# TensorE's instructions kept in the order of the program, from the first to the last

## The chip, the cores and the metric

The kernel runs on one core of a Trainium2 chip. The metric is device microseconds per execution, and lower is better. The kernel before takes 317.19 us, the median of 3 runs (316.95 to 317.62).

## The reference

One decoder layer on 256 tokens of width 1024, in float32. One input projection feeds two groups of eight heads of width 64. Group A is stick-breaking attention, group B a dilated sliding-window softmax attention whose three windows are merged by their denominators. Every head's output is RMS-normalised with a gain; an output projection, a residual and a LayerNorm follow, then a SwiGLU feed-forward of inner width 2816 with a second residual and LayerNorm.

```python
proj = jnp.einsum('bsd,dn->bsn', h, w_in[l])
q_a, k_a, v_a, q_b, k_b, v_b = jnp.split(proj, split_at, axis=-1)
o_a = stick_breaking_attention(_heads(q_a), _heads(k_a), _heads(v_a))
o_b = dilated_window_attention(_heads(q_b), _heads(k_b), _heads(v_b), slopes)
mixed = jnp.concatenate([_head_rms_merge(o_a, g_sb[l]), _head_rms_merge(o_b, g_dil[l])], axis=-1)
h = _layer_norm(ALPHA * h + jnp.einsum('bsm,md->bsd', mixed, w_out[l]), ln1_g[l], ln1_b[l])
gate = jnp.einsum('bsd,df->bsf', h, w_gate[l])
up = jnp.einsum('bsd,df->bsf', h, w_up[l])
ffn = jnp.einsum('bsf,fd->bsd', jax.nn.silu(gate) * up, w_down[l])
h = _layer_norm(ALPHA * h + ffn, ln2_g[l], ln2_b[l])
```

## The kernel before

**Products.** Every operand of a projection is split in two parts, `hi` (rounded to the matmul's own type, by ScalarE) and `lo` (the rest, by VectorE); `split` at line 78 does that. A product is three matmuls, hi by hi, hi by lo and lo by hi (`prod`, line 223). Weights come in chunks of 128x2048, which the class `Weights` loads and splits a piece at a time between other work: the tiles `wraw`, `whi` and `wlo` in the trace.

**Stages.** Heads are worked in eight pairs. Pairs 0 to 3 are group A, pairs 4 to 7 group B. `qk_proj` projects queries and keys of one pair into a PSUM bank with tag `in` (the tile `p_in`), and `v_proj` projects values into banks with the same tag. There are two such banks, used in turn. `evacuate` (line 253) copies the bank out: ScalarE writes `padhi` twice and `oh`, VectorE writes `padlo` twice and `ol`, which is the last reader. Then come scores, weights, values (line 363, the tile `o`) and `normalise` (line 384), which makes `mh` and `ml`, the pair's part of the output projection's input. The output projection of the first 128 tokens adds up in `acc0`, two banks with tag `in` (line 525), that of the other 128 in `acc1`, two banks with tag `big`. The first bank of `acc0` takes the place of pair 6's `p_in`, the second that of pair 7's. A LayerNorm of 128 tokens (`norm1`, line 567) is transposed on TensorE (tile `tr`, two rounds of four) for the feed-forward. The first three feed-forward chunks are computed by token (`ff_by_token`, line 617) and their gated product is transposed (tile `pt`); the rest by channel. The down projection and the second LayerNorm end the kernel.

**What sets the order.** The program is not written stage after stage: a small planner, the class `Order` (line 408), keeps a clock of its own while the program is traced. `fill` emits one product of a long projection and adds its cost; a follow-up step (scores, weights, values, normalise, transposes) is queued with a lag by `after` and emitted by the first `fill` at which its time has come. `drain` emits what is left. That gives the order of the program. After it, the framework's scheduler arranges each engine's instructions by its own estimate of when they are ready. It leaves alone those marked by `tc.keep_in_program_order`. The class `Pinned` (line 62) marks what is issued through `pe`, `act_e` and `dve`, while its class variable `on` holds: `step1` (line 454) clears it once scores of a pair other than 0 are emitted, so at pair 1's. From there the scheduler is free. Instructions written as `nc.tensor...`, such as the stick-breaking weights' (line 311), the transposes' and the values', are never marked.

```python
            return lambda *a, **k: tc.keep_in_program_order(f(*a, **k)) if Pinned.on else f(*a, **k)

            x1 = scores(j, pad, plain)
            Pinned.on = Pinned.on and j == 0
```

Of the kernel before, what the change touches and what calls it, by code (L numbers as in the profile page):

```python
# [47 lines left out]
def decoder_layer(ctx: ExitStack, tc: tile.TileContext, first, x, wqk, wv, wo, wgu, wd,  # L48
                  gmix, lnrows, biases, out):
    nc = tc.nc  # L50
# [11 lines left out]
    class Pinned:  # L62

        on = True

        def __init__(self, engine):
            self.engine = engine

        def __getattr__(self, name):
            f = getattr(self.engine, name)  # L70
            return lambda *a, **k: tc.keep_in_program_order(f(*a, **k)) if Pinned.on else f(*a, **k)  # L71

    pe, act_e, dve = Pinned(nc.tensor), Pinned(nc.scalar), Pinned(nc.vector)

    def bank(tag, name):
        return ps.tile([128, 512], F32, tag=tag, name=name)

    def split(src, hi, lo):
        act_e.activation(hi, src, AF.Copy)
        dve.tensor_sub(lo, src, hi)  # L80
# [93 lines left out]
    for i in range(4):  # L174
        r = wp.tile([128, 2048], F32, tag="wraw", name="wraw", bufs=NRAW)
# [5 lines left out]
    idle = cst.tile([128, 128], BF16, name="idle")  # L181
    nc.vector.memset(idle, 0.0)
    warm = bank("o", "warm")
    for _ in range(NWARM):
        nc.tensor.matmul(warm.rearrange("p (r n) -> p r n", r=4), idle,  # L185
                         idle[:, None, :].to_broadcast([128, 4, 128]), start=True, stop=True, skip_group_check=True)


# [2 lines left out]
    ident = cst.tile([128, 128], F32, name="ident")  # L191
    identb = cst.tile([128, 128], BF16, name="identb")
    maskb = cst.tile([128, 128], BF16, name="maskb")
    blkr = cst.tile([128, 128], F32R, name="blkr")
# [10 lines left out]
    for h in range(2):  # L205
        r = slice(h * 64, h * 64 + 64)
# [16 lines left out]
    def prod(dst, lhs, rhs, start, stop):  # L223

        pe.matmul(dst, lhs[0], rhs[0], start=start, stop=False, skip_group_check=True)
        pe.matmul(dst, lhs[0], rhs[1], start=False, stop=False, skip_group_check=True)
        pe.matmul(dst, lhs[1], rhs[0], start=False, stop=stop, skip_group_check=True)
# [45 lines left out]
    def heads(t, n):  # L273
        return t[:, :2 * n].rearrange("p (h n) -> p h n", h=2)
# [30 lines left out]
    def stick_weights(z0, z1, sph, spl):  # L305
        z0d = z0.rearrange("p (h n) -> p h n", h=2)
        for sp in (sph, spl):
            s1 = sp[:, 512:768]
            for dst, lhs, rhs in ((z0, negtri, sp[:, 0:512]), (z0d[:, :, 128:256], negones, heads(s1, 128)),
                                  (z1[:, :256], negtri, s1)):  # L310
                nc.tensor.matmul(dst, lhs, rhs, start=False, stop=True, skip_group_check=True)  # L311
        w0 = at.tile([128, 512], F32, tag="w0", name="w0")
        w1 = at.tile([128, 256], F32, tag="w1", name="w1")
        nc.scalar.activation(w0, z0, AF.Exp)
        nc.scalar.activation(w1, z1[:, :256], AF.Exp)
        return w0, w1
# [32 lines left out]
    def dilated_weights(e0, e1):  # L349
        t0 = bank("big", "t0")  # L350
        t1 = bank("sml", "t1")
        for h in range(2):
            nc.tensor.transpose(t0[:, h * 256:h * 256 + 128], e0[:, h * 128:h * 128 + 128], ident)
        for h in range(2):
            nc.tensor.transpose(t0[:, h * 256 + 128:h * 256 + 256], e1[:, h * 256:h * 256 + 128], ident)
            nc.tensor.transpose(t1[:, h * 128:h * 128 + 128], e1[:, h * 256 + 128:h * 256 + 256], ident)
        w0 = at.tile([128, 512], F32, tag="w0", name="w0")
        w1 = at.tile([128, 256], F32, tag="w1", name="w1")
        nc.scalar.activation(w0, t0, AF.Copy)
        nc.vector.tensor_copy(w1, t1[:, :256])  # L360
        return w0, w1

    def values(j, w0, w1):

        g, pj = divmod(j, 4)
        o = bank("o", "o")
        for h in range(2):
            c = slice(pj * 128 + h * 64, pj * 128 + h * 64 + 64)
            r = slice(h * 64, h * 64 + 64)
            nc.tensor.matmul(o[r, 0:256], vt[g, 0][:, c], w0[:, h * 256:h * 256 + 256],  # L370
                             start=True, stop=False, skip_group_check=True)
        for h in range(2):
            c = slice(pj * 128 + h * 64, pj * 128 + h * 64 + 64)
            r = slice(h * 64, h * 64 + 64)
            nc.tensor.matmul(o[r, 128:256], vt[g, 1][:, c], w1[:, h * 128:h * 128 + 128],  # L375
                             start=False, stop=True, skip_group_check=True)
        sq = at.tile([128, S], F32, tag="sq", name="sq")
        nc.scalar.activation(sq, o[:, :S], AF.Square)
        sqh = at.tile([128, 2, S], F32R, tag="sqh", name="sqh")
        nc.scalar.activation(sqh[:, 0, :], o[:, :S], AF.Square)  # L380
        nc.vector.tensor_sub(sqh[:, 1, :], sq, sqh[:, 0, :])
        return o, sqh

    def normalise(j, o, sq):

        ms = o[:, S:2 * S]
        for i in range(2):
            nc.tensor.matmul(ms, blkr, sq[:, i, :], start=i == 0, stop=i == 1, skip_group_check=True)  # L388
        sq = at.tile([128, S], F32, tag="sq", name="sq")
        nc.scalar.activation(sq, ms, AF.Ln, bias=eps_rms)  # L390
        nc.scalar.activation(sq, sq, AF.Exp, scale=-0.5)
        nc.vector.scalar_tensor_tensor(sq, o[:, :S], gm[:, j:j + 1], sq, op0=ALU.mult, op1=ALU.mult)
        mh = cst.tile([128, S], F32R, tag=f"m{j}0", name="mh")
        ml = cst.tile([128, S], F32R, tag=f"m{j}1", name="ml")
        split(sq, mh, ml)
        mixed[j] = (mh, ml)
# [69 lines left out]
    vt, v_at = {}, {}  # L466
# [100 lines left out]
    def norm1(t, acc, lag):  # L567
        def after(c, h):
            n = c.start // 512

            def transposes():
                p = bank("sml", "tr")
                for i in range(4):
                    kt = n * 4 + i
                    nc.tensor.transpose(p[:, i * 128:i * 128 + 128],  # L575
                                        h[:, kt * 128:kt * 128 + 128], ident)
                pv = p.rearrange("p (k n) -> p k n", k=4)
                hi = xhi[:, n * 4:n * 4 + 4, t * 128:t * 128 + 128]
                lo = xlo[:, n * 4:n * 4 + 4, t * 128:t * 128 + 128]
                nc.scalar.activation(hi, pv, AF.Copy)  # L580
                nc.vector.tensor_sub(lo, pv, hi)
            od.after(lag + n * 0.66, 0.43, transposes)
        return layer_norm(acc, x_nat[:, t, :], rows1[:, 0, :], rows1[:, 1, :], x_nat[:, t, :], after, halves)
# [9 lines left out]
    def gated(g, u, shape, tag, dst=None):  # L593
        s = ff.tile(shape, F32, tag=tag, name="silu", bufs=3)
        nc.scalar.activation(s, g, AF.Silu)
        if dst is None:
            dst = s
        else:
            s, u = (v.rearrange("p (t n) -> p t n", t=2) for v in (s, u))
        nc.vector.tensor_mul(dst, s, u)  # L600
        return dst
# [15 lines left out]
    def ff_by_token(f, t, tag, last):  # L617
        w = weights.get(14 + f)
        tk = slice(t * 128, t * 128 + 128)
        p = bank(tag, "pg")  # L620
        for kt in range(KT):
            c = slice(kt * 256, kt * 256 + 256)
            od.fill(0.33, lambda: prod(p[:, :256], (xhi[:, kt, tk], xlo[:, kt, tk]), (w[0][:, c], w[1][:, c]),
                                       kt == 0, kt == KT - 1))
        with tc.issue_after(last):
            a = gated(p[:, 0:128], p[:, 128:256], [128, 128], "at")

        def transpose():
            q = bank("sml", "pt")
            nc.tensor.transpose(q[:, :128], a, ident)  # L630
            nc.scalar.activation(act[f][0][:, tk], q[:, :128], AF.Copy)
            nc.vector.tensor_sub(act[f][1][:, tk], q[:, :128], act[f][0][:, tk])
        od.after(LAG_ACT, 0.11, transpose)
# [195 lines left out]
```

## Time and profile before

| | before |
|---|---|
| median of 3 runs | 317.19 us |
| the profiled execution's own time | 316.86 us |
| its span, first to last instruction | 315.1 us |
| TensorE busy | 305.9 us, 97%, 2112 matmuls |
| VectorE busy | 240.6 us, 76% |
| ScalarE busy | 190.7 us, 61% |
| TensorE's share of the chain that ended last | 94% |
| mean granted clock of TensorE | 0.996 |

TensorE (PE in the rows) works through nearly the whole span. VectorE (DVE) and ScalarE (ACT) prepare its operands. Times in the rows count from the start of the span. A timeline row gives the start and the time of an instruction until its result is there; matmuls of a row overlap, so the next one starts earlier than the row before it ends. An "x2" behind a row means that two instructions, which follow each other closely, are shown as one.

### The profile page before, as it was taken

How to read it: one execution, taken by the hardware profiler on the slowest of the kernel's cores; microseconds unless marked ns; L12 is line 12 of the kernel's file. 1: busy time of each engine (PE TensorE's matmuls, PEld its weight loads, DVE VectorE, ACT ScalarE, POOL GpSimd, SP SyncE). 2: the span in 40 equal slices, each digit the busy share in tenths (PEclk: the TensorE clock that was granted, in tenths of full speed). 3: DMA queues.
4: the chain of work that ended last, by engine and by line, in shares of the span. 5: the costliest groups of instructions: out<-in, count | busy, mean ns of one | idle time of the engine just before them, and what ended most of it. 6: DMA issues, size and time to landing. Idle time of an engine off the chain costs nothing.

```text
span 315.1 us, 5440 instructions
## 1 busy us (share of the span) xinstructions
PE 305.9 (97%) x2112; PEld 277.8 (88%) x2112; DVE 240.6 (76%) x465; ACT 190.7 (61%) x406; POOL 4.1 (1%) x22
## 2 busy tenths in 40 slices
PE   8999999999999999999999999999999999999990
PEld 4988898799997778999999999999999988888880
DVE  4778998659897479997646466585597699999765
ACT  5789997777787458666446364473542675565011
POOL 5000000000000000000000000000000000000000
PEclk9999999999999999999999999999999999999998
DMA  7979887297332104789455464563613253630011
GB/s 255 399 301 381 277 283 263 113 358 292 151 137 69 64 2 133 249 294 370 157 189 214 139 226 172 166 235 133 218 50 136 80 188 130 270 135 0 0 67 67
DMA packets 9657, 58.02 MB, mean 184 GB/s; under 512 B 1184, under 2 KB 1440, under 8 KB 3360
## 3 DMA queue, kind: packets, MB, share of 16 engines
q1 hardware_dynamic: 9344, 57.22, 49.8%
q10 hardware_dynamic: 288, 0.46, 0.4%
q8 instruction: 16, 0.26, 0.3%
q14 instruction: 9, 0.07, 0.1%
HBM read 56.63 MB, written 1.05 MB: 183 GB/s over the span
## 4 chain that ended last, share of the span: by engine, by line
PE 94%; DVE 2%; ACT 1%; DMA 1%; issue 0%; DVEq 0%
PE pg L71 40%; PE p_in L71 22%; PE d L71 15%; PE acc L71 7%; PE z L71 2%; PE o L370 1%; PE s L71 1%; PE warm L185 1%; PE z L311 1%; DVE y L563 1%; PE o L375 1%; DVE bst L548 1%; DMA out_h<-y 1%; DVE y L546 1%; PE o L388 1%; PE tr L575 1%
## 5 line engine op out<-in xcount | busy, mean ns | idle before, releaser
L71 DVE TENSOR_TENSOR wlo<-wraw,whi 128x512 fp32r<-128x512 f32 (+2 forms) x194 | 138.0, 739 | 37.9 <-ACT whi L71 37.0
L71 ACT ACTIVATE whi<-wraw 128x512 fp32r<-128x512 f32 (+2 forms) x194 | 121.2, 671 | 58.0 <-PE pg L71 35.2
L71 PE MATMUL pg<-xhi,whi 128*128 128x256 f32 x304 | 85.7, 282 | 0.0
L71 PE MATMUL pg<-xlo,whi 128*128 128x256 f32 x304 | 85.5, 281 | 0.0
L71 PE MATMUL pg<-xhi,wlo 128*128 128x256 f32 x304 | 85.5, 281 | 0.0
L71 PEld LDWEIGHTS pg<-xhi,whi 128*128 128x128 f32 x304 | 57.2, 188 | 0.0
L71 PEld LDWEIGHTS pg<-xlo,whi 128*128 128x128 f32 x304 | 57.2, 188 | 0.0
L71 PEld LDWEIGHTS pg<-xhi,wlo 128*128 128x128 f32 x304 | 57.2, 188 | 0.0
L71 PE MATMUL p_in<-xhi,whi 128*128 128x256 f32 x128 | 36.5, 286 | 0.0
L71 PE MATMUL p_in<-xhi,wlo 128*128 128x256 f32 x128 | 36.3, 283 | 0.0
L71 PE MATMUL p_in<-xlo,whi 128*128 128x256 f32 x128 | 36.1, 282 | 0.0
L71 PE MATMUL d<-whi,s 128*128 128x512 f32 x84 | 26.9, 395 | 0.0
L71 PE MATMUL d<-whi,a 128*128 128x512 f32 (+1 forms) x92 | 25.9, 363 | 0.0
L71 PEld LDWEIGHTS p_in<-xhi,whi 128*128 128x128 f32 x128 | 24.1, 188 | 1.4 <-issue 0.7
L71 PEld LDWEIGHTS p_in<-xlo,whi 128*128 128x128 f32 x128 | 24.1, 188 | 0.2
L71 PEld LDWEIGHTS p_in<-xhi,wlo 128*128 128x128 f32 x128 | 24.1, 188 | 0.1
L71 PEld LDWEIGHTS d<-whi,s 128*128 128x128 f32 x84 | 15.8, 188 | 3.8
L71 PEld LDWEIGHTS d<-whi,a 128*128 128x128 f32 x92 | 16.6, 189 | 2.9
L71 PE MATMUL d<-wlo,a 128*128 128x512 f32 (+1 forms) x46 | 16.7, 363 | 0.0
L71 PE MATMUL d<-wlo,s 128*128 128x512 f32 x42 | 16.6, 395 | 0.0
L71 ACT ACTIVATE s<-slots 128x896 fp32r<-128x896 f32 x6 | 5.7, 953 | 13.4 <-DVE slots L611 13.4
L71 PE MATMUL pg<-wlo,xhi 128*128 128x256 f32 x48 | 13.6, 286 | 0.0
(151 smaller groups left out, 473.7 us busy)
## 6 DMA issues: line engine op xcount, KB each, us to landing
wraw<-in_wgu SPq DMA_DIRECT2D x22, 1024.0 KB, 4.8
wraw<-in_wd SPq DMA_DIRECT2D x11, 1024.0 KB, 4.8
wraw<-in_wqk SPq DMA_DIRECT2D x6, 1024.0 KB, 5.7
wraw<-in_wo SPq DMA_DIRECT2D x4, 1024.0 KB, 4.7
wraw<-in_first SPq DMA_DIRECT2D x8, 384.0 KB, 6.3
wraw<-in_wv SPq DMA_DIRECT2D x3, 1024.0 KB, 5.4
rows<-in_lnrows SPq DMA_DIRECT2D x2, 1024.0 KB, 6.6
wraw<-in_wv SPq DMA_DIRECT2D x2, 512.0 KB, 7.0
```

The lines of the kernel that those rows point to most:

```text
L71: return lambda *a, **k: tc.keep_in_program_order(f(*a, **k)) if Pinned.on else f(*a, **k)
L185: nc.tensor.matmul(warm.rearrange("p (r n) -> p r n", r=4), idle, idle[:, None, :].to_broadcast([128, 4, 128]), start=True, stop=True, ski ...
L311: nc.tensor.matmul(dst, lhs, rhs, start=False, stop=True, skip_group_check=True)
L370: nc.tensor.matmul(o[r, 0:256], vt[g, 0][:, c], w0[:, h * 256:h * 256 + 256], start=True, stop=False, skip_group_check=True)
L375: nc.tensor.matmul(o[r, 128:256], vt[g, 1][:, c], w1[:, h * 128:h * 128 + 128], start=False, stop=True, skip_group_check=True)
L388: nc.tensor.matmul(ms, blkr, sq[:, i, :], start=i == 0, stop=i == 1, skip_group_check=True)
L546: nc.vector.scalar_tensor_tensor(y[:, c], res[:, c], scale, acc[i][:, :c.stop - c.start], op0=ALU.mult, op1=ALU.add)
L548: nc.vector.bn_stats(st[:, i, :], y[:, c])
L563: nc.vector.scalar_tensor_tensor(dst[:, c], y[:, c], r[:, 3:4], b[:, c], op0=ALU.mult, op1=ALU.add)
L575: nc.tensor.transpose(p[:, i * 128:i * 128 + 128], h[:, kt * 128:kt * 128 + 128], ident)
```

## The change

`Pinned` takes a second argument, `always`. TensorE's wrapper is made with it, so it marks each instruction whatever `Pinned.on` says. ScalarE's and VectorE's wrappers are as before. The matmuls and transposes that were written as `nc.tensor...` are written as `pe...`. No instruction is added or taken away, and no lag or cost of the planner is changed. ScalarE's and VectorE's unmarked instructions are still arranged by the scheduler, which now arranges them around another order on TensorE.

```diff
-        def __init__(self, engine):
+        def __init__(self, engine, always=False):
             self.engine = engine
+            self.always = always
 
         def __getattr__(self, name):
             f = getattr(self.engine, name)
-            return lambda *a, **k: tc.keep_in_program_order(f(*a, **k)) if Pinned.on else f(*a, **k)
-
-    pe, act_e, dve = Pinned(nc.tensor), Pinned(nc.scalar), Pinned(nc.vector)
+            return lambda *a, **k: tc.keep_in_program_order(f(*a, **k)) if self.always or Pinned.on else f(*a, **k)
+
+    pe, act_e, dve = Pinned(nc.tensor, True), Pinned(nc.scalar), Pinned(nc.vector)
...
-                nc.tensor.matmul(dst, lhs, rhs, start=False, stop=True, skip_group_check=True)
+                pe.matmul(dst, lhs, rhs, start=False, stop=True, skip_group_check=True)
...
-            nc.tensor.matmul(ms, blkr, sq[:, i, :], start=i == 0, stop=i == 1, skip_group_check=True)
+            pe.matmul(ms, blkr, sq[:, i, :], start=i == 0, stop=i == 1, skip_group_check=True)
...
-            nc.tensor.transpose(q[:, :128], a, ident)
+            pe.transpose(q[:, :128], a, ident)
```

The other lines of the diff put `pe` for `nc.tensor` in the same way: the idle matmuls at the start, the transposes of the dilated weights, the values and the transposes of the first LayerNorm.

**Place one: pair 1's stick-breaking weights, on TensorE.** `sph` and `spl` are the two parts of the logarithms, written by VectorE; `p_in_410` is the value projection of the second 128 tokens and `p_in_469` pair 2's projection. A number behind a name tells tiles of one name apart, and the square brackets name the engines whose work an instruction waits for. Before:

```order
L71 MATMUL p_in_410<-whi_321,xlo_72 128x512
L311 MATMUL z0_368<-sph_378,negtri_99 128x512 [waits DVE_49]
L311 MATMUL z0_368<-sph_378,negones_98 128x2x128
L311 MATMUL z1_369<-sph_378,negtri_99 128x256
L71 MATMUL p_in_410<-whi_321,xhi_71 128x512
L71 MATMUL p_in_410<-wlo_322,xhi_71 128x512
L71 MATMUL p_in_410<-whi_321,xlo_72 128x512
L71 MATMUL p_in_469<-xhi_71,whi_364 128x256 [waits Activation_49]
L71 MATMUL p_in_469<-xlo_72,whi_364 128x256
L311 MATMUL z0_368<-spl_379,negtri_99 128x512 [waits DVE_49]
L311 MATMUL z0_368<-spl_379,negones_98 128x2x128
L311 MATMUL z1_369<-spl_379,negtri_99 128x256
```

The same stretch of TensorE in the changed kernel:

```order
L72 MATMUL p_in_410<-whi_321,xlo_72 128x512
L72 MATMUL z0_368<-sph_378,negtri_99 128x512 [waits DVE_49]
L72 MATMUL z0_368<-sph_378,negones_98 128x2x128
L72 MATMUL z1_369<-sph_378,negtri_99 128x256
L72 MATMUL z0_368<-spl_379,negtri_99 128x512 [waits DVE_49]
L72 MATMUL z0_368<-spl_379,negones_98 128x2x128
L72 MATMUL z1_369<-spl_379,negtri_99 128x256
L72 MATMUL p_in_410<-whi_321,xhi_71 128x512
L72 MATMUL p_in_410<-wlo_322,xhi_71 128x512
L72 MATMUL p_in_410<-whi_321,xlo_72 128x512
```

The six matmuls stand together now, and the group on `sph` stands three matmuls of 128x512 further ahead than before. The five matmuls that stood between the two groups come after both.

**Place two: the start of the output projection, on TensorE.** `acc0_1236` and `acc0_1237` are the two banks of the first 128 tokens, `mh_528` and `mh_541` the normalised pairs 0 and 1, `t0_1256` the transposes of pair 6's weights and `s0_1278` pair 7's scores. Before:

```order
L71 MATMUL acc0_1236<-whi_1027,mh_528 128x512 [waits PE_49]
...
L71 MATMUL acc0_1236<-whi_1027,mh_541 128x512
...
L353 MATMUL t0_1256<-ident_100,e_1179 128x128 [waits DVE_49,PE_49]
...
L370 MATMUL o_1302<-w0_1264,v10_727 64x256 [waits Activation_49]
...
L375 MATMUL o_1302<-w1_1265,v11_786 64x128 [waits DVE_49]
L71 MATMUL s0_1278<-padhi1_281,oh_1228 128x256 [waits PE_49,Activation_49]
...
L71 MATMUL acc0_1237<-whi_1027,mh_528 128x512 [waits DVE_49,PE_49]
...
L71 MATMUL s0_1278<-padhi1_281,ol_1229 128x256
L71 MATMUL s1_1279<-padhi1_281,ol_1229 128x512
L375 MATMUL o_1302<-w1_1265,v11_786 64x128
```

The same stretch of TensorE in the changed kernel:

```order
L72 MATMUL acc0_1236<-whi_1027,ml_529 128x512
L72 MATMUL acc0_1237<-whi_1027,mh_528 128x512 [waits DVE_49,PE_49]
...
L72 MATMUL acc0_1236<-whi_1027,mh_541 128x512
...
L72 MATMUL t0_1256<-ident_100,e_1179 128x128 x3
...
L72 MATMUL s0_1278<-padhi1_281,oh_1228 128x256 [waits Activation_49]
...
L72 MATMUL o_1302<-w0_1264,v10_727 64x256 [waits Activation_49]
```

The first matmul of `acc0_1237` is now the fourth of the stage, ahead of pair 6's transposes and pair 7's scores; it was the twenty-fourth. Groups that were cut in two (pair 7's scores, pair 6's values) stand whole.

**Place three: the end of the output projection of the first 128 tokens, on TensorE.** `mh_1367` and `mh_1408` are the normalised pairs 6 and 7, `o_1385` pair 7's values and, with `blkr`, its mean of squares; `acc1` is the other 128 tokens. Before:

```order
L71 MATMUL acc0_1237<-whi_1315,ml_1275 128x512
L370 MATMUL o_1385<-w0_1357,v10_727 64x256 [waits Activation_49]
...
L71 MATMUL acc1_1416<-whi_1027,mh_528 128x512 [waits PE_49]
...
L71 MATMUL acc1_1417<-whi_1027,mh_528 128x512 [waits PE_49]
L71 MATMUL acc0_1236<-whi_1342,mh_1367 128x512 [waits Activation_49]
...
L388 MATMUL o_1385<-sqh_1392,blkr_103 128x256 [waits DVE_49]
L71 MATMUL acc1_1417<-wlo_1028,mh_528 128x512
...
L71 MATMUL acc1_1416<-whi_1145,mh_808 128x512
L71 MATMUL acc0_1236<-whi_1342,mh_1408 128x512 [waits Activation_49]
```

The same stretch of TensorE in the changed kernel:

```order
L72 MATMUL acc0_1237<-whi_1315,ml_1275 128x512
L72 MATMUL acc0_1236<-whi_1342,mh_1367 128x512 [waits Activation_49]
...
L72 MATMUL acc0_1236<-whi_1342,ml_1368 128x512 [waits DVE_49]
L72 MATMUL o_1385<-w0_1357,v10_727 64x256 x2
...
L72 MATMUL o_1385<-sqh_1392,blkr_103 128x256 [waits DVE_49]
L72 MATMUL acc0_1236<-whi_1342,mh_1408 128x512 [waits Activation_49]
...
L72 MATMUL acc1_1416<-whi_1027,mh_528 128x512 [waits PE_49]
```

Thirteen matmuls of `acc1` stood between pair 7's values and the first matmul on `mh_1408`, four of them ahead of the one on `mh_1367`. All of them stand behind `acc0` now, and `mh_1367` is wanted ahead of pair 7's values. Further on, TensorE's transposes of the first LayerNorm stand 14 matmuls of 128x512 earlier than before, and the transposes `pt` of the first three feed-forward chunks stand where the planner put them, that of the third chunk right behind the chunk's last product.

## Rows read from the trace of the kernel before

**Rows 1.** Chain of waits, whole span; columns: start, length, what ran, how many.

```profile
29.37 2.10 PE p_in L71 x9
...
107.78 0.22 PE o L375 x4
...
123.32 7.72 PE pg L71 x65
...
145.18 105.02 PE pg L71 x885
```

**Rows 2.** Timeline of TensorE, pair 1's weights; start, time, line, output<-inputs.

```profile
31.31 0.40 PE L311 MATMUL z<-sph,negtri 128*128 128x512 f32 x1
...
32.71 0.39 PE L311 MATMUL z<-spl,negtri 128*128 128x512 f32 x1
```

**Rows 3.** Timeline of VectorE, the two parts of pair 1's logarithms.

```profile
30.17 0.55 DVE L301 CAST sph<-ab 128x768 fp32r<-128x768 f32 x1
...
31.24 0.95 DVE L302 TENSOR_TENSOR spl<-ab,sph 128x768 fp32r<-128x768 f32 x1
```

**Rows 4.** Timeline of TensorE, start of the output projection; brackets: idle before, releaser.

```profile
94.11 0.39 PE L71 MATMUL acc<-whi,mh 128*128 128x512 f32 x1
...
97.21 0.65 PE L370 MATMUL o<-w,v 128*64 128x256 f32 x4 [0.22 <-ACT w L359]
...
100.62 0.43 PE L375 MATMUL o<-w,v 128*64 128x128 f32 x2
```

**Rows 5.** Timeline of ScalarE, pair 7's evacuation.

```profile
97.41 0.39 ACT L71 ACTIVATE oh<-p_in 128x256 fp32r<-128x256 f32 x1
```

**Rows 6.** Timeline of VectorE, pair 7's evacuation.

```profile
96.56 0.43 DVE L71 SCALAR_TENSOR_TENSOR padlo<-p_in,padhi 64x256 fp32r<-64x256 f32 x1
...
97.48 0.69 DVE L71 TENSOR_TENSOR wlo<-wraw,whi 128x512 fp32r<-128x512 f32 x1
98.09 0.42 DVE L71 SCALAR_TENSOR_TENSOR ol<-p_in,oh 128x256 fp32r<-128x256 f32 x1
```

**Rows 7.** Timeline of TensorE, pairs 6 and 7 at the projection's end.

```profile
106.80 0.39 PE L71 MATMUL acc<-whi,ml 128*128 128x512 f32 x1
...
107.61 0.39 PE L375 MATMUL o<-w,v 128*64 128x128 f32 x4
...
110.36 0.41 PE L388 MATMUL o<-sqh,blkr 128*128 128x256 f32 x2
```

**Rows 8.** Timeline of ScalarE, pair 7's normalised part.

```profile
112.28 0.42 ACT L71 ACTIVATE mh<-sq 128x256 fp32r<-128x256 f32 x1 [0.55 <-DVE sq L392]
```

**Rows 9.** Timeline of VectorE, normalising pairs 6 and 7.

```profile
107.63 0.48 DVE L392 SCALAR_TENSOR_TENSOR sq<-o,gm,sq 128x256 f32<-128x256 f32 x1 [0.91 <-ACT sq L391]
...
109.10 0.42 DVE L381 TENSOR_TENSOR sqh<-sq,sqh 128x256 fp32r<-128x256 f32 x1
...
112.73 0.42 DVE L71 TENSOR_TENSOR ml<-sq,mh 128x256 fp32r<-128x256 f32 x1 [0.48 <-ACT mh L71]
```

**Rows 10.** Timeline of VectorE, the second half's first LayerNorm and first gated product.

```profile
124.53 0.66 DVE L546 SCALAR_TENSOR_TENSOR y<-x_nat,acc 128x512 f32<-128x512 f32 x1
...
126.92 0.20 DVE L550 BATCH_NORM_AGGREGATE mv<-bst 128x2 f32<-128x12 f32 x1
...
128.92 1.41 DVE L563 SCALAR_TENSOR_TENSOR x_nat<-y,rs,rows 128x512 f32<-128x512 f32 x2
130.33 0.49 DVE L600 TENSOR_TENSOR silu<-silu,pg 128x128 f32<-128x128 f32 x2
```

**Rows 11.** Timeline of ScalarE, one gate of the feed-forward.

```profile
136.19 0.28 ACT L595 ACTIVATE silu<-pg 128x128 f32<-128x128 f32 x1 [0.67 <-PE pg L71]
```

**Rows 12.** Windows: length, each engine's busy time, granted clock (PEclk), DMA share, GB/s.

```profile
307.30:312.30 5.00, 0.00 (x0) 0.00 (x0) 4.38 (x10) 1.46 (x6) 0.00 (x0) 1.00 0.05 20
312.40:315.00 2.60, 0.00 (x0) 0.00 (x0) 0.00 (x0) 0.00 (x0) 0.00 (x0) 0.50 0.43 149
```

**Rows 13.** Timeline of TensorE, the idle matmuls at the start.

```profile
1.05 4.35 PE L185 MATMUL warm<-idle 128*128 128x512 bf16 x10 [1.05 <-DVE idle L182]
```

More of the change, by code (lines that the diff above doesn't have):

```diff
@@ L184, in decoder_layer @@
     for _ in range(NWARM):
-        nc.tensor.matmul(warm.rearrange("p (r n) -> p r n", r=4), idle,
+        pe.matmul(warm.rearrange("p (r n) -> p r n", r=4), idle,
                          idle[:, None, :].to_broadcast([128, 4, 128]), start=True, stop=True, skip_group_check=True)
@@ L352, in dilated_weights @@
         for h in range(2):
-            nc.tensor.transpose(t0[:, h * 256:h * 256 + 128], e0[:, h * 128:h * 128 + 128], ident)
+            pe.transpose(t0[:, h * 256:h * 256 + 128], e0[:, h * 128:h * 128 + 128], ident)
         for h in range(2):
-            nc.tensor.transpose(t0[:, h * 256 + 128:h * 256 + 256], e1[:, h * 256:h * 256 + 128], ident)
-            nc.tensor.transpose(t1[:, h * 128:h * 128 + 128], e1[:, h * 256 + 128:h * 256 + 256], ident)
+            pe.transpose(t0[:, h * 256 + 128:h * 256 + 256], e1[:, h * 256:h * 256 + 128], ident)
+            pe.transpose(t1[:, h * 128:h * 128 + 128], e1[:, h * 256 + 128:h * 256 + 256], ident)
         w0 = at.tile([128, 512], F32, tag="w0", name="w0")
@@ L369, in values @@
             r = slice(h * 64, h * 64 + 64)
-            nc.tensor.matmul(o[r, 0:256], vt[g, 0][:, c], w0[:, h * 256:h * 256 + 256],
+            pe.matmul(o[r, 0:256], vt[g, 0][:, c], w0[:, h * 256:h * 256 + 256],
                              start=True, stop=False, skip_group_check=True)
@@ L374, in values @@
             r = slice(h * 64, h * 64 + 64)
-            nc.tensor.matmul(o[r, 128:256], vt[g, 1][:, c], w1[:, h * 128:h * 128 + 128],
+            pe.matmul(o[r, 128:256], vt[g, 1][:, c], w1[:, h * 128:h * 128 + 128],
                              start=False, stop=True, skip_group_check=True)
@@ L574, in transposes @@
                     kt = n * 4 + i
-                    nc.tensor.transpose(p[:, i * 128:i * 128 + 128],
+                    pe.transpose(p[:, i * 128:i * 128 + 128],
                                         h[:, kt * 128:kt * 128 + 128], ident)
```

## The prediction

> **What bounds the kernel now.** I read the chain of waits first. For 105 us after 145.18, 885 feed-forward matmuls follow one another with nothing between them [rows 1], and the chain reads so nearly all the way from the first projection to the second LayerNorm. TensorE is the bound, and it hardly waits for anyone: the longest idle time that its timeline names is 0.22 us [rows 4]. From that follows how the change is costed. No matmul is added or removed, so TensorE's work is the same, and since it has no slack, a microsecond that it waits longer is a microsecond on the end. I then set the two orders side by side, and at each place where an instruction came forward I read when its operand was there and when TensorE would now reach it.
>
> A matmul of 128x512 takes 0.23 us on TensorE (nine in 2.10), one of 128x256 in the feed-forward 0.119 (65 in 7.72) [rows 1]. An operand's result is handed over some 0.05 us after the writer's row ends; that is my estimate, from gaps of 0.03 to 0.05 between such rows.
>
> **Place one, pair 1's weights.** The matmuls on `sph` began at 31.31 [rows 2]; three matmuls of 128x512 earlier is 31.31 - 0.69 = 30.62. VectorE ends `sph` at 30.17 + 0.55 = 30.72 [rows 3], so TensorE waits until 30.77: 0.15. The three matmuls on `sph` take 0.47 (one of 128x512, two of half the width), which brings it to 31.24. `spl` ends at 31.24 + 0.95 = 32.19 [rows 3], handed over at 32.24: a wait of 1.00. Before, five other matmuls stood in that gap and the first on `spl` came at 32.71 [rows 2], when it was ready. VectorE's list up to `spl` is the same in both orders, so this chain doesn't move. Cost **1.15**, from 1.1 to 1.4: the upper end is for pair 0's and 1's normalisation, in front of which the scheduler now puts one or two more weight pieces on VectorE.
>
> **Place two, the second bank.** `acc0_1237` takes the bank that pair 7's projection left, so it waits for the last reader, `ol` on VectorE. The stage begins at 94.11 [rows 4]; after three matmuls TensorE reaches it at 94.80. When is `ol` done? Before, at 98.09 + 0.42 = 98.51 [rows 6], with `oh` at 97.41 [rows 5], because pair 6's copies stood in front. In the new order ScalarE does `oh` ahead of them, and VectorE's list is: second `padlo`, one weight piece, `ol`. The second `padlo` starts at 96.56 and ends at 96.99; the weight piece takes 0.61 to the next start (97.48 to 98.09), so `ol` runs from about 97.5 to 97.95 [rows 6]. Wait: 98.0 - 94.8 = **3.2**. Bounds: 2.6 if `ol` follows `padlo` at once (97.4), 3.7 if it ends where it did.
> Something is given back here. Behind the wait all operands are ready: pair 6's transposes come 3.2 us later than their weights need, and so do the scores. TensorE's wait for pair 6's copy `w` goes, 0.22 us [rows 4] and about 0.15 for resuming. The groups that were cut in two are whole: two lone value matmuls took 0.36 to 0.43 [rows 4], where four in one group take 0.22 [rows 1]. That makes 0.5; more switches of operand kind may add as much. I take 0.7, out of 0.2 to 1.0. Net **2.5**, from 1.6 to 3.5.
>
> **Place three, pairs 6 and 7.** Three waits, counted on the clock of before.
> First, `mh_1367` is wanted right after pair 5's part: at 106.80 + 0.23 = 107.03 [rows 7]. VectorE's step before it ends at 107.63 + 0.48 = 108.11 [rows 9]; `mh` adds 0.42 [rows 8], so 108.58 with the handovers: a wait of 1.55. `ml` comes 0.45 behind [rows 8, 9], just when two matmuls have run.
> Second, pair 7's mean of squares needs both halves of `sqh`. Before, VectorE wrote the second 109.10 + 0.42 - 107.61 = 1.9 us after the last value matmuls began [rows 7, 9], with pair 6's `mh` and `ml` in between. Those are out of the way, which saves some 0.4, while TensorE has only three matmuls and the first half (1.2 us) to fill in: a wait of 0.35, from 0.2 to 0.7.
> Third, `mh_1408` follows at once. From the row on 110.36 to the end of `mh`, 112.28 + 0.42, are 2.34 us [rows 7, 8]; the two matmuls of that row take 0.24 of it: a wait of 2.1. Its `ml` (112.73 + 0.42) [rows 9] is again no later than the third matmul.
> Together 4.0. The 13 `acc1` matmuls that covered these waits run afterwards and cover nothing. Before, `mh_1408` was itself awaited for about 0.2, which goes. Net **3.8**, from 3.3 to 4.4.
> The first LayerNorm's transposes come 14 matmuls earlier, and I looked for a wait there. With 30 `acc1` matmuls (6.9 us) behind `acc0`'s end, TensorE reaches them at about 115.0 + 6.9 = 121.9. The second half's `y` comes at about 115.3, and from `y` to the last step took 4.4 us in the other LayerNorm (124.53 to 128.92), which gives 0.7 a half [rows 10]: ready by 120.4 and 121.1. No cost; the cover is 0.8 us.
>
> **Place four, the transposes `pt`.** The feed-forward starts 3.8 later in this stretch. Its 51 matmuls ahead of the first `pt` take 6.07, so TensorE reaches it at about 133.0. The chain behind it (LayerNorm, table load, gate, product) began with `y` at 124.53 and its product ended at about 130.6 [rows 10]. `acc1` now ends at about 127.1, and `y` starts there or one weight piece later; I take 127.6, a shift of 3.07, hence 133.7: a wait of **0.7**, from 0.2 to 1.4.
> The third chunk's `pt` stands right behind its own product. The gate starts when that matmul's result is there and takes 0.28 [rows 11], the product 0.25 [rows 10]; the result comes about 0.28 after the matmul starts, my estimate after the 0.39 to 0.40 of the wider shape [rows 2]. With handovers that is 0.93, less the matmul's own 0.12: a wait of **0.8**, up to 1.4 if VectorE is inside a weight piece.
>
> **Sum.** 1.15 + 2.5 + 3.8 + 0.7 + 0.8 = 8.95. Later stages give nothing back: TensorE runs through them without a pause [rows 1], and the order from there to the end is the same. On the profiled execution's 316.86 that is 325.8. The median of the runs lies 0.33 above that execution, so I forecast **326.1**, with an own range of 324.0 to 328.0 from the terms' ends, which won't all fall on one side.
>
> **Rivals.**
> *The clock falls in a wait.* The idle matmuls at the start, of the 128x512 shape, took 4.35 us for ten where full rate needs 2.3 [rows 13]: such a restart costs 2.0. For it speaks that place two leaves TensorE idle for 3.2 us and place three for two more waits within 5 us. Against it: after the last matmul the granted clock was still at its upper level, 2.4 GHz, through 5 us in which TensorE did nothing, and only then at 0.50, 1.2 GHz [rows 12]. One such fall gives 328.1. The Trainium skill (TensorE: Matmul & The Clock Gate, "Part 1: The HAM clock gate") says that the low rate is the default and that activity lifts it; by that rule a long enough wait returns the low rate. The trace agrees that it returns, and shows it only after a longer pause than any wait forecast here.
> *The other engines come sooner.* They are arranged anew, and while TensorE waits they get ahead with weights. If the `pt` products are there in time, `ol` follows `padlo` closely and the whole groups save 1.0, the sum is 1.15 + 1.6 + 3.8 = 6.55: 323.7. For it: VectorE and ScalarE have idle time in the later half. Against it: the long chains begin with TensorE's own output (the projection, the values, the mean of squares), so a lead in weights doesn't shorten them.
> *Not slower: the cut groups decide.* If all operands were there when reached, only the saving of place two would remain, and the time would be 317.2 - 1.0 = 316.2. This decides if `ol` ends by 94.8 instead of 97.95 and `mh_1367` by 107.0 instead of 108.6. Only an evacuation over 3 us shorter could do that, and its rows are back to back.
> *Nothing changes.* The order would have to be undone on the chip; then 317.2. Nothing in the trace shows TensorE taking a matmul ahead of a waiting one: at 97.21 it sat idle with `acc` matmuls behind [rows 4].
>
> **How the numbers follow.** Forecast 0.71, clock 0.11, sooner 0.13, not slower 0.04, nothing 0.01. Within 0.2% (0.6 us), about what a measurement of this kernel can tell from no change, I put 0.02, as much as "nothing" and the near part of "not slower" make; faster 0.03; slower 0.95. The range of 8 in 10 runs from 323.6, which takes in the second rival, to 328.6, which takes in one fall of the clock.
>
> **What would show it.** In the profile after: TensorE's timeline has idle time ahead of the first `spl` matmul of pair 1 (about 1.0), ahead of the second `acc` bank (3.2, released by VectorE's `ol`), ahead of the first `mh` of pairs 6 and 7 (1.5 and 2.1, released by ScalarE) and ahead of two `pt` (0.7 and 0.8). TensorE's busy time stays within 1 us of what it was, the feed-forward runs without a pause from some 9 us later on, and the stretch from its last matmul to the end is as before. I am wrong if the second bank isn't awaited at all, if the granted clock drops between 94 and 140 us, or if the time lost by 145 is not found again at the end.

## The result, and the profile after

The changed kernel takes **329.41 us**, the median of 4 runs (328.61 to 330.30), beside 317.31 us for the kernel before: slower by the factor 1.0387 (95% interval 1.0372 to 1.0401). The forecast was 326.1 and its range ended at 328.6. The profiled execution took 330.3 us, its span is 328.6.

The page's first part shows that TensorE is no longer busy nearly all the time (97% before). Its busy time also rose, by 4.6 us, where the prediction wanted it within 1 us:

```profile
PE 310.5 (94%) x2112; PEld 280.2 (85%) x2112; DVE 241.9 (74%) x465; ACT 191.2 (58%) x406; POOL 4.1 (1%) x22
```

TensorE's waits are grouped by what was awaited; the columns are the total in us, how often, and the longest. Before, only the idle matmuls at the start (1.1) and one `w` (0.2) stood here:

```profile
PE acc L72 <- ACT mh L72: 3.4, 2, 2.0
PE acc L72 <- DVE ol L72: 3.3, 1, 3.3
PE pt L72 <- DVE silu L601: 1.1, 2, 0.7
PE warm L72 <- DVE idle L183: 1.0, 1, 1.0
PE z L72 <- DVE spl L303: 0.7, 1, 0.7
PE p_in L72 <- DVE ol L72: 0.4, 1, 0.4
```

Every forecast wait of half a microsecond or more is here, with the releaser that was forecast: `ol` for place two, two `mh` for place three, two `silu` for place four, `spl` for place one. The two small ones (0.15 on `sph`, 0.35 on pair 7's mean of squares) are not rows of their own. The last row is none of them: the first value projection came 0.53 later than before, in a stretch whose order is the same in both kernels.

How far the changed kernel is behind can be read at instructions that both kernels have. In the timeline of TensorE after, these are the first value projection, the first product of the output projection, the first transpose of pair 7 and the first product of the feed-forward; the two rows on `sph` and `spl` are place one:

```profile
17.71 0.47 PE L72 MATMUL p_in<-whi,xhi 128*128 128x512 f32 x1 [0.44 <-DVE ol L72]
...
31.31 0.49 PE L72 MATMUL z<-sph,negtri 128*128 128x512 f32 x1
...
32.78 0.50 PE L72 MATMUL z<-spl,negtri 128*128 128x512 f32 x1 [0.74 <-DVE spl L303]
...
96.02 0.39 PE L72 MATMUL acc<-whi,mh 128*128 128x512 f32 x1
...
111.61 0.38 PE L72 MATMUL t<-ident,e 128*128 128x128 f32 x2
...
135.03 0.29 PE L72 MATMUL pg<-whi,xhi 128*128 128x256 f32 x1
```

The output projection began at 94.11 before [rows 4]; the other three stand in the timeline of before:

```profile
17.18 0.47 PE L71 MATMUL p_in<-whi,xhi 128*128 128x512 f32 x1
...
105.44 0.38 PE L353 MATMUL t<-ident,e 128*128 128x128 f32 x2
...
123.16 0.28 PE L71 MATMUL pg<-whi,xhi 128*128 128x256 f32 x1
```

The last one is in the chain of waits after, the long run of the feed-forward (`pg`), which began at 145.18 before [rows 1]:

```profile
158.64 105.02 PE pg L72 x885
```

The lag grows to 1.91 by the output projection (0.53 of it at the start, 1.38 in place one), then by 4.26 across place two, by 5.70 across place three and by 1.59 across place four: 13.46 in all. From there nothing is lost or found again (885 matmuls in 105.02 us in both), and the span is 13.5 longer. Places one and four cost about what was forecast (1.15 and 1.5). Places two and three cost 4.26 and 5.70 where 2.5 and 3.8 were forecast. The timeline of TensorE at place two shows why:

```profile
96.49 0.40 PE L72 MATMUL acc<-whi,ml 128*128 128x512 f32 x1
100.23 0.76 PE L72 MATMUL acc<-whi,mh 128*128 128x512 f32 x1 [3.35 <-DVE ol L72]
100.80 0.63 PE L72 MATMUL acc<-wlo,mh 128*128 128x512 f32 x1
101.22 0.63 PE L72 MATMUL acc<-whi,ml 128*128 128x512 f32 x1
...
103.65 0.39 PE L72 MATMUL acc<-whi,ml 128*128 128x512 f32 x1
```

Behind the wait of 3.35 the same matmuls start 0.42 apart instead of 0.23. From 100.23 to 103.65 eight of them run, in 3.42 us where 1.84 would do: about 1.6 lost. The windows of after say what that is (length, busy time of TensorE, of its weight load, VectorE, ScalarE and GpSimd, then the granted clock):

```profile
96.90:100.00 3.10, 0.00 (x0) 0.00 (x0) 2.95 (x6) 2.54 (x6) 0.00 (x0) 1.00 0.00 0
100.20:103.40 3.20, 3.17 (x8) 2.52 (x9) 0.48 (x1) 0.00 (x0) 0.00 (x0) 0.50 0.47 138
103.60:111.00 7.40, 7.40 (x43) 5.82 (x43) 4.04 (x18) 3.97 (x14) 0.00 (x0) 1.00 0.17 72
...
117.90:120.10 2.20, 0.25 (x1) 0.05 (x1) 0.48 (x1) 1.30 (x3) 0.00 (x0) 1.00 0.00 0
120.50:123.80 3.30, 3.30 (x9) 2.57 (x8) 1.75 (x4) 0.00 (x0) 0.00 (x0) 0.51 0.02 5
124.00:130.00 6.00, 6.00 (x28) 4.90 (x27) 5.35 (x10) 4.55 (x13) 0.00 (x0) 1.00 0.00 0
```

The granted clock fell to 0.50, 1.2 GHz, twice: just before place two's wait ended, and again just after TensorE had resumed behind place three's. There two waits stood within seven microseconds:

```profile
114.78 0.50 PE L72 MATMUL acc<-whi,mh 128*128 128x512 f32 x1 [1.42 <-ACT mh L72]
...
120.13 0.50 PE L72 MATMUL acc<-whi,mh 128*128 128x512 f32 x1 [1.98 <-ACT mh L72]
121.24 0.63 PE L72 MATMUL acc<-whi,mh 128*128 128x512 f32 x1
...
123.80 0.46 PE L72 MATMUL acc<-whi,mh 128*128 128x512 f32 x1
```

From 120.13 to 123.80 nine matmuls take 3.67 instead of 2.07: again 1.6. By this count the waits themselves cost 2.7 in place two and 4.1 in place three, and the two falls 3.2.

### The profile page after: what moved, and what is told of

Same layout as the page of the kernel before. It is cut to its first block, busy times and chain, and to the rows that moved or that the text cites. A ratio compares the mean times of both kernels' runs of the same rounds, so it can differ in the third digit from the quotient of the medians.

```text
span 328.6 us, 5444 instructions
## 1 busy us (share of the span) xinstructions
PE 310.5 (94%) x2112; PEld 280.2 (85%) x2112; DVE 241.9 (74%) x465; ACT 191.2 (58%) x406; POOL 4.1 (1%) x22
## 4 chain that ended last, share of the span: by engine, by line
PE 77%; DVE 11%; ACT 5%; DMA 4%; issue 2%; DVEq 0%
PE pg L72 36%; PE p_in L72 15%; PE d L72 15%; PE acc L72 5%; DVE wlo L72 3%; PE o L72 2%; DMA wraw<-in_wv 2%; PE z L72 2%; ACT whi L72 2%; PE s L72 1%; DMA wraw<-in_first 1%; DVE y L547 1%; DVE bst L549 1%; DVE x_nat L564 1%; PE t L72 1%
## 5 line engine op out<-in xcount | busy, mean ns | idle before, releaser
L72 PE MATMUL acc<-whi,mh 128*128 128x512 f32 x32 | 14.4, 451 | 6.7 <-ACT mh L72 3.4
L553 ACT ACTIVATE rs<-mv,eps_ln 128x1 f32<-128x1 f32 x4 | 1.2, 296 | 24.0 <-DVE mv L551 24.0
```

Of the source, the lines that this page charges most:

```text
L553: nc.scalar.activation(r[:, 0:1], mv[:, 1:2], AF.Ln, bias=eps_ln)
```

## The experiments

Theory: each wait costs about its length, and on top of that the clock falls behind places two and three, 1.6 or so each time. Rivals: the extra is something else (transfers, VectorE and ScalarE arranged anew), or one sequence on TensorE costs something by itself.

**Idle matmuls in the waits.** The waits stay, but TensorE computes something nobody reads while it waits (`busy` issues so many matmuls of 128x512 on idle data).

```diff
...
+        if j == NPAIR - 2:
+            spare = bank("sml", "spare")
+            busy(spare, 6)
         for n in range(2):
+            if j == 0 and n == 1:
+                busy(bank("big", "spare"), 13)
             od.fill(0.65, lambda: out_step(acc0, 0, j, n))
     od.drain()
+    busy(spare, 8)
```

> The changed kernel with 27 idle matmuls of 128x512 added on TensorE, which write to a spare PSUM bank and compute nothing: 13 behind the first product of the output projection (in front of the wait for the second bank), 6 in front of pair 6's part and 8 in front of pair 7's part. The order and every wait's end stay; only what TensorE does while it waits is changed. Theory (the two falls of the granted clock are what the sum missed): the clock stays at its upper level from 94 to 140 us, the matmuls behind the two waits take 0.23 us instead of 0.43, and the time is that of the changed kernel less two falls at 1.7 us each, 326.9 us on its profiled execution, 326.4 to 327.4, with every run alike. Rival (the waits themselves are longer than forecast and the clock is only a companion): the time stays at 329.4 us or above, whatever the clock does. Second rival (27 more matmuls cost what they take): 329.4 + 27 x 0.23 = 335.6 us.

Measured: 328.98 us (327.96 to 329.71), before beside it 317.33. That misses the theory's range by 1.6 and lies 0.4 under the rival's 329.4. The profile did what the theory said in the middle of the kernel: its granted clock was full to the last matmul. But an output transfer in its chain of waits was long; in the changed kernel's chain that row reads 2.06. The first two rows are the first product of the output projection, from the timeline, and the long run:

```profile
96.33 0.39 PE L72 MATMUL acc<-whi,mh 128*128 128x512 f32 x1
...
156.04 105.03 PE pg L72 x885
...
314.46 4.04 DMA out_h<-y
```

That is 2.0 of the profiled execution's 329.71; whether the other three had it too isn't known. So the same kernel was run again beside the changed one.

> The changed kernel as it is, once more, on the chip of the runs below. Theory (two falls of the granted clock at 1.7 us each, behind the waits of places two and three, that do not come in every execution): the times spread over some 1.7 to 3.4 us and go with the mean granted clock, 328.6 at 0.989 (one fall) and 330.3 at 0.985 (two), and below 327.5 only where the clock is 0.993 or more. Rival (the extra 3.3 us are the transfers of the output or something else that is not the clock): times and mean clock do not go together.

> The changed kernel with 27 matmuls on idle data (their results are read by nobody) put into the waits of places two and three, a second time, because the profile of the first showed no fall of the clock but an output transfer of 4.04 us where before took 2.06. Theory: the clock stays at full speed to the last matmul, and without the long transfer the time is 327.0 to 328.0, that is 1.5 to 2.4 below the changed kernel beside it. Rival (the clock's falls cost nothing that the waits do not cost already): within 0.6 of the changed kernel.

Measured: the changed kernel 329.86 (328.51 to 330.01), the filled one **327.86** (327.29 to 329.52; ratio to before 1.0347, 1.0323 to 1.0371), before 317.06. The eight runs of the changed kernel fall into two groups that go with the clock: five at 329.8 to 330.3 us with a mean clock of 0.981 to 0.985, three at 328.5 to 328.9 with 0.989. Only the two profiled ones, both of the first group, show the falls themselves, two in each. One fall in each of the three others would fit but isn't shown: the mean also counts the stretch at 0.50 after the last matmul, which lasted 2.6 us in the profile of before [rows 12] and 6.0 in that of the first filled kernel, whose mean was 0.991 with no fall before it:

```profile
322.00:328.00 6.00, 0.00 (x0) 0.00 (x0) 2.62 (x5) 1.12 (x5) 0.00 (x0) 0.50 0.25 87
```

In the second filled profile the granted clock is full through places two and three and to the last matmul:

```profile
96.00:100.00 4.00, 3.47 (x16) 1.46 (x15) 3.55 (x7) 2.96 (x7) 0.00 (x0) 1.00 0.00 0
100.00:104.00 4.00, 4.00 (x25) 3.16 (x25) 1.14 (x6) 1.31 (x4) 0.00 (x0) 1.00 0.62 223
113.00:118.00 5.00, 4.85 (x24) 2.34 (x23) 1.13 (x3) 1.85 (x5) 0.00 (x0) 1.00 0.01 3
118.50:124.00 5.50, 5.50 (x25) 4.43 (x24) 4.82 (x9) 1.87 (x7) 0.00 (x0) 1.00 0.00 0
124.00:321.00 197.00, 192.07 (x1372) 180.30 (x1370) 149.39 (x247) 101.59 (x187) 0.00 (x0) 1.00 0.44 158
```

And in its timeline the matmuls behind the wait are at full speed, with most of the wait filled:

```profile
17.24 0.47 PE L72 MATMUL p_in<-whi,xhi 128*128 128x512 f32 x1
...
95.54 0.39 PE L72 MATMUL acc<-whi,mh 128*128 128x512 f32 x1
...
96.24 2.98 PE L72 MATMUL spare<-idle 128*128 128x512 bf16 x13
99.75 0.47 PE L72 MATMUL acc<-whi,mh 128*128 128x512 f32 x1 [0.53 <-DVE ol L72]
```

Its long run, in its chain of waits:

```profile
155.26 105.03 PE pg L72 x885
```

And the same two rows of the changed kernel's second profile:

```profile
95.72 0.39 PE L72 MATMUL acc<-whi,mh 128*128 128x512 f32 x1
...
158.14 105.03 PE pg L72 x885
```

Work that computes nothing made the kernel 2.0 us faster beside the changed one. All nine runs of the filled kernel against all eight of the changed one give 1.8 (328.08 and 329.86), and the two sets overlap. The profiles are clearer. From the first product of the output projection to the long run of the feed-forward, both filled profiles take 59.7 us (155.26 - 95.54 and 156.04 - 96.33), and both of the changed kernel 62.6 and 62.4 (158.64 - 96.02 and 158.14 - 95.72). The waits end as late in both kernels: the second bank's 4.21 after that product, and place three's last 7.6 after the first product behind pair 7's transposes. So what is saved is the falls. The slower filled runs without a profile, from 328.94 to 329.52 at 0.989 to 0.993, stay unexplained.

**Place two alone, and place three alone.** In the first, the first bank's products of pairs 0 to 4 come ahead of the second bank's, so that `ol` has time, and pair 7's scores are queued 0.97 later. In the second, products of the other 128 tokens (`acc1`) stand in place three's waits, and pair 7's values come ahead of pair 6's products; `ahead` issues so many products of `acc1`.

```diff
...
-    for j in range(NPAIR - 1):
+    for j, n in [(j, n) for js in ((0, 1, 2, 3, 4), (5,), (6,)) for n in range(2) for j in js]:
         while j not in mixed:
             od.drain(len(od.steps) - 1)
-        for n in range(2):
-            od.fill(0.65, lambda: out_step(acc0, 0, j, n))
+        od.fill(0.65, lambda: out_step(acc0, 0, j, n))
```

> The changed kernel with another order of the output projection in the program: the first bank's products of pairs 0 to 4, then the second bank's, and pair 7's scores one product later. So the second bank is wanted some 4 us later, after its last reader. Theory (a wait of 3.3 us and the fall of the clock behind it): both go, 2.6 + 1.7 = 4.3 us off a run that has both falls; 325.0 to 326.2 us for the median, the wait for VectorE's ol under 0.5 us, the granted clock at its upper level from 96 to 115 us, and the second fall, in place three, still there. Rival (the wait alone, no clock): 329.4 - 2.6 = 326.8 us, and matmuls at 0.43 us still stand behind the start of the projection.

```diff
...
+    while NPAIR - 1 not in valued:
+        od.run(min(od.steps, key=lambda s: s[0]))
+    ahead(1)
+    for n in range(2):
+        out_step(acc0, 0, NPAIR - 2, n)
     od.drain()
+    ahead(3)
...
```

> The changed kernel with products of the other 128 tokens written into the waits at the end of the first 128 tokens' output projection: one ahead of pair 6's part, three ahead of pair 7's, and pair 7's values ahead of pair 6's part. Theory: the waits of 1.4 and 2.0 us for ScalarE's mh go, the 0.4 us at pair 7's mean of squares as well, and with them the second fall of the clock: 4.0 + 1.7 = 5.7 us off a run that has both falls, 323.4 to 324.8 us for the median; the first fall, behind the wait for the second bank, stays. Rival (no clock): 329.4 - 4.0 = 325.4 us.

Measured: 325.67 (325.39 to 326.44) and 325.53 (323.75 to 326.70), before 317.33. The first lies in the theory's range. The second misses it by 0.7 and is the number of the rival without a clock (325.4), so its time alone would speak against the theory. But in its profile each kernel kept the fall of the place that it left. With place two covered, TensorE's windows show the fall in place three only:

```profile
116.20:119.40 3.20, 3.20 (x9) 2.53 (x9) 1.86 (x3) 0.00 (x0) 0.00 (x0) 0.50 0.02 5
119.60:126.00 6.40, 6.40 (x32) 5.31 (x31) 5.73 (x10) 5.08 (x14) 0.00 (x0) 1.00 0.00 0
```

With place three covered, the fall behind place two lasted twice as long in the profiled execution, the slowest of the four. Of the 5.67 busy at half rate some 2.8 are lost, by my estimate, not 1.6, which accounts for 1.2 of that execution's miss; how long the fall was in the other three isn't known. The first row is the wait itself, from the timeline:

```profile
100.13 0.77 PE L72 MATMUL acc<-whi,mh 128*128 128x512 f32 x1 [3.36 <-DVE ol L72]
...
99.10:105.80 6.70, 5.67 (x17) 4.73 (x18) 1.62 (x4) 0.69 (x2) 0.00 (x0) 0.50 0.43 157
105.90:112.00 6.10, 6.10 (x33) 4.65 (x33) 3.77 (x18) 3.60 (x14) 0.00 (x0) 1.00 0.00 0
```

**Both places.** The two edits together, with the step behind pair 7's scores queued 0.97 sooner after them.

> The waits of places two and three covered by products of the out-projection (the first accumulator's bank in full before the second, and products of the second token block between the last pair's steps), places one and four left as the change has them. Theory: with the waits their falls of the clock go too, and what is left is 1.4 (place one), 1.6 (place four) and some 0.4 at the start over before: 320.0 to 321.2. Rival (the falls come from the fixed order as such, wherever the waits are): 323.4 or more, with the clock at 0.5 somewhere before the last matmul.

Measured: **320.10** (319.94 to 320.27), before 317.06. The clock is full throughout the stretch, and the four runs agree within 0.33 us:

```profile
95.90:125.00 29.10, 28.99 (x149) 22.44 (x148) 20.94 (x50) 19.41 (x50) 0.00 (x0) 1.00 0.22 76
```

The fixed order alone doesn't make the clock fall. Against this kernel, set off from before in each case, place three alone costs 8.34 - 3.04 = 5.3 and place two alone 8.20 - 3.04 = 5.2. With the 3.04 that is 13.5, more than the 12.1 and 12.8 by which the medians of the changed kernel lie over before: the places don't add up exactly, and the fall behind place two, longer in the kernel with place three covered, is one reason that the traces show.

**All four places, twice.** Pair 1's weights are queued 1.3 later, the first `pt` 1.4 later, and `drain(1)` leaves the third chunk's `pt` queued, to be issued among the next products:

```diff
...
-            od.after(lags[1], 0.9 if a_kind else 0.65, step2)
+            od.after(lags[1] + (1.3 if j == 1 else -0.97 if j == 7 else 0.0), 0.9 if a_kind else 0.65, step2)
...
-        od.after(LAG_ACT, 0.11, transpose)
+        od.after(LAG_ACT + (1.4 if f == 0 and t == 0 else 0.0), 0.11, transpose)
...
-    od.drain()
+    od.drain(1)
```

> All four places mended in the order of the program, TensorE pinned throughout as in the changed kernel: pair 1's weights later by two products, the second bank later, products of the other 128 tokens in the waits of place three, the first pt later and the third not drained. Theory (the loss is these waits and the falls behind them, and nothing else of the change costs): back to the kernel before, less its own waits and cut groups of 0.7 to 1.0 us: 316.5 us, 315.8 to 317.4, with the granted clock at its upper level to the last matmul. Rival (a fixed order costs something by itself, such as the scheduler's list for ScalarE and VectorE): 318 us or more.

Measured: 318.49 (318.37 to 318.68), before 317.33, ratio 1.0040 (1.0025 to 1.0055): a miss by 1.1 over the range, on the rival's side. TensorE's waits name the place. The first `pt`, queued 1.4 later, was behind the transposes of the LayerNorm now and waited for VectorE's `xlo`:

```profile
PE pt L72 <- DVE xlo L600: 1.0, 1, 1.0
```

So it was moved once more, behind 12 further matmuls, which are four products (the diff has 3.0 for 1.4).

> All four places covered as in the kernel of 318.49, and the first transpose of a silu product put 12 products later. There it waited 0.98 for VectorE behind the transposes of the second token block (1.33 us from the end of these to its start). Theory (what was left over before was that wait and the start's jitter): 317.0 to 317.6, no different from before. Rival (keeping one sequence costs something by itself): 318.2 or more.

Measured: **317.38** (317.07 to 317.99, 11 runs), before 317.06, ratio 1.0008 (0.9999 to 1.0016): no difference from before. In this kernel TensorE keeps the program's order from the first to the last instruction. The waits that its trace groups are two, at the start:

```profile
PE warm L72 <- DVE idle L183: 1.0, 1, 1.0
PE p_in L72 <- ACT whi L72: 0.5, 1, 0.5
```

The rival that one sequence costs something by itself is out, to within the interval's upper end of 0.5 us.

**Place four left.** The last kernel without the two edits of place four.

> Places one, two and three covered, place four alone left as the change has it: between the kernel of 320.1 (places one and four left) and that of 317.38 (none left). Theory (each wait costs its own length, whichever others are there): place four alone costs 1.3 to 1.6 over the kernel with all four covered, 318.6 to 319.0, and place one is then worth 1.1 to 1.5 of the 2.7. Rival (the later start of the out-projection behind place one is taken up again by the waits that follow it, so that place one costs nothing at the end): 319.8 to 320.2.

Measured: 319.23 (319.04 to 319.36), 0.2 over the theory's range in absolute time, and before 317.38 beside it, 0.3 more than in the run above. Above before that is 1.85; all four covered 0.32, places one and four left 3.04. So place four costs 1.53 and place one 1.19: both differences as the theory has them, and the later start behind place one isn't taken up by later waits. TensorE's waits in this trace are the two `silu`:

```profile
PE pt L72 <- DVE silu L619: 1.5, 2, 0.8
```

## Why the prediction failed

*Place one* (1.15): 1.38 in the profile of after, 1.19 between kernels. Right. Three matmuls of 0.47 from 31.31 leave 1.00 up to 32.78, as forecast; the 0.74 in brackets counts from the end of the row before and so reads less.

*Place two* (3.2 less 0.7): the wait is 3.35 by the bracket, 3.51 counted as in the forecast (96.49 + 0.23 to 100.23), and without the fall the stretch lost 2.7, for a net 2.5. Right in mechanism and size. VectorE's `ol` did come behind `padlo` and one weight piece.

*Place three* (3.8): 4.1 without the fall. Right; waits of 1.42 and 1.98 for 1.55 and 2.1, the 0.35 on the mean of squares shows as 0.84 for its two matmuls where another pair's took 0.48, and the first LayerNorm's transposes waited for nobody.

*Place four* (1.5): 1.59 in the profile, 1.53 between kernels. Right in sum; the waits that the profile names are 0.40 and 0.69, less than forecast, and the other 0.5 is not named.

The sum of these steps was 8.95 and is 9.8. The profiled execution adds 0.53 at the start, which doesn't go with the change: with the same order there, the other profiles began the value projection anywhere from 17.20 (the kernel of 317.38) to 18.02 (the first filled one).

*The step that failed* is the rival "the clock falls in a wait": it was kept out of the sum, held at 0.11 and priced at one fall, with "shows it only after a longer pause than any wait forecast here". I had one pause in the trace, the one after the last matmul, in which the clock held for 5 us [rows 12], and read it as the least pause that brings a fall. It was only one pause that long. The prediction's own sign of being wrong, a granted clock that drops between 94 and 140, came true twice. In the changed kernel the clock fell between 100.00 and 100.20, inside place two's wait of 3.35, and behind place three's with no pause over 2 us. With place three covered it was down by 99.10, 2.3 us into the same wait (100.13 - 3.36 = 96.77). Yet in the changed kernel's own execution it again held for over 4 us after the last matmul, with TensorE idle throughout:

```profile
320.80:325.30 4.50, 0.00 (x0) 0.00 (x0) 4.22 (x10) 1.46 (x6) 0.00 (x0) 1.00 0.00 0
```

So the length of a pause alone didn't decide whether the clock fell. Why it fell sooner in one wait than in another stayed open. The Trainium skill (TensorE: Matmul & The Clock Gate, "Part 1: The HAM clock gate") says that the number of matmuls at the low rate at the start of a kernel varies from run to run. The changed kernel's two traces agree, in mid-kernel and by little: behind place two, eight matmuls from 100.23 to 103.65 in the first, seven from 99.93 to 102.94 in the second.

The price per fall, 2.0, was near the 1.6 measured. The count was not: the rival had one fall, the kernel has two places for one, and both profiled executions took both. 326.1 and two falls at 2.0 would have been 330.1, the upper group of the runs. With the falls kept out by idle matmuls the time is 327.9 in the second set, within the forecast's own range, and 328.98 in the first, with the long transfer in its profile. The other rivals are answered too. At the second bank and at pairs 6 and 7 the awaited operands came no sooner than forecast by more than 0.2 us. The cut groups didn't decide, since whole groups on TensorE without waits are only as fast as before (317.38). And the order was kept on the chip.

## What to carry to other kernels

In this kernel TensorE was the bound: fixing its order cost nothing by itself, and leaving an instruction ahead of its operand cost about the whole wait. Pin an order only after each place where it moves something forward has been given work to stand in the gap. A wait on TensorE can have a second price behind it, matmuls at half rate. Here it followed the wait of 3.4 us, and the waits of 1.4 and 2.0 close together; single waits of 1.0 and less had none. Whether one wait of 2 us would have been enough wasn't tried. A pause that once passed without a fall is no bound: count the places where a fall could come and put their sum into the range.

## What the runs showed that was not expected

Idle matmuls whose result is thrown away save time where TensorE must wait anyway: 2.0 us between medians for 27 of them, 1.8 over all runs. The stretch at the low rate behind place two held 8 matmuls in the changed kernel's profile and 17 in the one with place three covered; what decides that stayed open. One output transfer took 2.06 us in the changed kernel's profile and 4.04 in one of the filled kernel, which hid most of the gain in that execution; why it was slow stayed open.

The granted clock of the windows doesn't show every stretch at half rate. The ten idle matmuls at the start took 4.35 us where full rate needs 2.3 [rows 13], the pace of the falls, yet the window over them reads 1.00. In the kernel before:

```profile
1.00:5.40 4.40, 4.35 (x12) 1.59 (x12) 0.58 (x2) 2.10 (x5) 3.73 (x17) 1.00 0.82 256
```

Behind places two and three the spacing of the matmuls shows the falls by itself. When the clock fell inside an idle stretch, and that it held after the last matmul, rests on that column alone.
